# Row normalization: two 8 MB tiles with 64 KiB per partition in place of four 4 MB tiles with 32 KiB, and one of four squares on VectorE

## The chip, the cores and the metric

The kernel runs on one core of one Trainium2 chip. The metric is the device time of one execution in microseconds (us), as a median over several runs. The span of a profile, from its first to its last instruction, is shorter than the measured time by 1.7 to 1.8 us.

## The reference

```python
# x: 1024 x 4096 float32, eps = 1e-12
norm = np.sqrt(np.sum(x ** 2, axis=-1, keepdims=True) + eps)
return (x / norm).astype(np.float32)
```

16.78 MB come in from HBM, the chip's main memory, and 16.78 MB go out to it. A row can be scaled only when it has been squared and summed as a whole.

## The kernel before

Four tiles of 128 partitions with two whole rows each. All loads are issued first, on the SP queue. Then for each tile ACT squares and sums two rows, ACT takes the square root, VectorE (DVE) takes the reciprocal and scales both rows in place, and SP issues the store. Each tile has its own buffer in SBUF, the on-chip memory, so nothing ever waits for a free one: the four loads are issued one behind the other, from 0.73 to 2.1 us.

```python
R = 2
n_tiles = N // (P * R)                       # 4
x = x.rearrange("(t p r) d -> t p (r d)", p=P, r=R)
...
for i in range(n_tiles):                     # all loads
    xt = io.tile([P, R, D], mybir.dt.float32)
    nc.sync.dma_start(out=xt.rearrange("p r d -> p (r d)"), in_=x[i])
    xts.append(xt)
for i in range(n_tiles):
    ...
    for r in range(R):
        nc.scalar.activation(out=sq, in_=xt[:, r], func=Square,
                             accum_out=ssq[:, r : r + 1])
    nc.scalar.activation(out=rstd, in_=ssq, func=Sqrt, bias=eps_t)
    nc.vector.reciprocal(out=rstd, in_=rstd)
    for r in range(R):
        nc.vector.tensor_scalar_mul(out=xt[:, r], in0=xt[:, r],
                                    scalar1=rstd[:, r : r + 1])
    nc.sync.dma_start(out=out_t[i], in_=xt.rearrange("p r d -> p (r d)"))
```

Of the kernel before, what the change touches and what calls it, by code (L numbers as in the profile page):

```python
# [1 line left out]

# [4 lines left out]


@with_exitstack  # L10
def kernel(
    ctx: ExitStack,
    tc: tile.TileContext,
    x: bass.AP,
    axis: bass.AP,
    eps: bass.AP,
    out: bass.AP,
):
    nc = tc.nc
    P = nc.NUM_PARTITIONS  # L20

    assert isinstance(axis, int) and axis in (-1, len(x.shape) - 1)
    eps = float(eps)

    x = x.flatten_outer_dims()
    out_flat = out.flatten_outer_dims()
    N, D = x.shape
    assert N % P == 0

    R = 2  # L30
    n_tiles = N // (P * R)
    x = x.rearrange("(t p r) d -> t p (r d)", p=P, r=R)
    out_t = out_flat.rearrange("(t p r) d -> t p (r d)", p=P, r=R)

    io = ctx.enter_context(tc.tile_pool(name="io", bufs=n_tiles))
    scratch = ctx.enter_context(tc.tile_pool(name="scratch", bufs=1))
    stats = ctx.enter_context(tc.tile_pool(name="stats", bufs=4))

    sq = scratch.tile([P, D], mybir.dt.float32)
    eps_t = scratch.tile([P, 1], mybir.dt.float32)  # L40
    nc.vector.memset(eps_t, eps)  # L41

    xts = []
    for i in range(n_tiles):
        xt = io.tile([P, R, D], mybir.dt.float32)
        nc.sync.dma_start(out=xt.rearrange("p r d -> p (r d)"), in_=x[i])  # L46
        xts.append(xt)

    for i in range(n_tiles):
        xt = xts[i]  # L50
        ssq = stats.tile([P, R], mybir.dt.float32)
        for r in range(R):
            nc.scalar.activation(  # L53
                out=sq,
                in_=xt[:, r],
                func=mybir.ActivationFunctionType.Square,
                accum_out=ssq[:, r : r + 1],
            )

        rstd = stats.tile([P, R], mybir.dt.float32)  # L60
        nc.scalar.activation(  # L61
            out=rstd,
            in_=ssq,
            func=mybir.ActivationFunctionType.Sqrt,
            bias=eps_t,
        )
        nc.vector.reciprocal(out=rstd, in_=rstd)  # L67

        for r in range(R):
            nc.vector.tensor_scalar_mul(  # L70
                out=xt[:, r], in0=xt[:, r], scalar1=rstd[:, r : r + 1]
            )
        nc.sync.dma_start(out=out_t[i], in_=xt.rearrange("p r d -> p (r d)"))


# [1 line left out]
_INS = ['x', 'axis', 'eps']  # L77
_OUTS = [((1024, 4096), 'float32')]
#: Inputs that are plain numbers.
_NUMBERS = {'axis': -1, 'eps': 9.999999960041972e-13}  # L80


# [26 lines left out]
```

## Time and profile before

| | before |
|---|---|
| time, median of the first 3 runs | 84.22 us (84.21 to 84.26) |
| span of the profile | 82.5 us |
| DMA packets | 1152, of which 1024 of 32 KiB |
| DMA busy, mean of 16 engines | 96% |
| ACT busy, DVE busy | 41%, 23% |
| loads landed | 13.04, 22.76, 32.48, 42.97 us |
| stores issued, first and last | 27.0 and 55.6 us |

The DMA row counts. Its 96% say that hardly anything but the transfer itself can set the time. A packet is here one partition's share of a tile, 32 KiB in one piece (4 tiles x 128 partitions, in and out, make 1024); such a piece is called a descriptor below. The other 128 packets have 4 bytes and take 9 ns; each of the eight transfers has 16 of them, at its end. They are called semaphore packets below. What is left to argue about is in single microseconds: the start, the end, and the place where loads give way to stores. For these no summary view is fine enough, and the single packet records of the trace were read as well: start, length and size of each packet on each engine. The lines of the views are shown in the prediction. The packet records stand in no view and don't name their engine: packets were strung together to 16 engines by the end of one and the start of the next.

### The profile page before, as it was taken

The page shows a single profiled execution, that of the slowest core. Times are in us where ns is not written, and L with a number is a line of the kernel's source. Part 1 is how long each engine was busy: PE and PEld are TensorE (multiplying, and loading weights), DVE is VectorE, ACT ScalarE, POOL GpSimd, SP SyncE. Part 2 cuts the span into 40 slices and gives each one's busy share as a digit, 9 for nine tenths or more (in the row PEclk, how much of TensorE's full clock was granted, in tenths as well). Part 3 has the DMA queues.
Part 4 walks back from the last instruction along what each step waited for, and adds up shares of the span by engine and source line. Part 5 has one row for each costly group of instructions (what it writes and reads, how often), then busy time and mean ns, then how long its engine had stood idle before and what let it go on. Part 6 is the DMA issues. An engine that isn't in the chain of part 4 may idle for free.

```text
span 82.5 us, 98 instructions
## 1 busy us (share of the span) xinstructions
DVE 19.2 (23%) x13; ACT 33.4 (41%) x22; POOL 0.2 (0%) x4
## 2 busy tenths in 40 slices
DVE  0000000000299019910498003990000000000000
ACT  6000006999799982999519996000000000000000
POOL 0000000000000000000000000000000000000000
DMA  6689998996999899899979989998998998899890
GB/s 175 286 365 445 508 397 365 508 461 302 508 493 397 381 508 413 350 508 461 302 302 461 493 381 397 508 413 350 508 445 381 445 508 381 381 508 413 365 493 0
DMA packets 1152, 33.55 MB, mean 407 GB/s; under 512 B 128, under 2 KB 128, under 8 KB 128
## 3 DMA queue, kind: packets, MB, share of 16 engines
q1 hardware_dynamic: 1152, 33.55, 96.0%
HBM read 16.78 MB, written 16.78 MB: 407 GB/s over the span
## 4 chain that ended last, share of the span: by engine, by line
DMA 50%; ACT 9%; DVE 3%; DVEq 3%; SPq 1%; issue 0%
DMA xt<-in_x_dram 50%; ACT sq L53 9%; DVE xt L70 3%; DVEq L104 3%; SPq L46 1%; ACT rstd L61 0%; DVE rstd L67 0%
## 5 line engine op out<-in xcount | busy, mean ns | idle before, releaser
L53 ACT ACTIVATE sq<-xt 128x4096 f32<-128x4096 f32 x8 | 28.9, 3617 | 16.5 <-DMA xt<-in_x_dram 16.4
L70 DVE TENSOR_SCALAR xt<-xt,rstd 128x4096 f32<-128x4096 f32 x8 | 18.5, 2350 | 0.1
L67 DVE RECIPROCAL rstd<-rstd 128x2 f32<-128x2 f32 x4 | 0.7, 166 | 35.5 <-ACT rstd L61 35.5
L53 ACT ACT_TABLE_LOAD x1 | 1.3, 1283 | 0.7 <-PEq L90 0.7
L53 ACT ACTIVATION_READ_ACCUMULATOR sq<-xt 128x1 f32 x8 | 1.5, 186 | 0.0
L61 ACT ACT_TABLE_LOAD x1 | 1.3, 1283 | 0.0
L61 ACT ACTIVATE rstd<-ssq,eps_t 128x2 f32<-128x2 f32 x4 | 1.2, 296 | 0.1
L41 DVE MEMSET eps_t<- 128x1 f32 x1 | 0.1, 59 | 0.8 <-PEq L90 0.8
L90 POOL MEMSET const-bfloat16-1.0<- 128x1 bf16 x1 | 0.1, 102 | 0.0
L90 POOL MEMSET const-uint8-127<- 128x1 uint8 x1 | 0.1, 102 | 0.0
L90 POOL MEMSET const-float32-0.0<- 128x1 f32 x1 | 0.1, 99 | 0.2 <-issue 0.2
L90 POOL MEMSET const-float32-1.0<- 128x1 f32 x1 | 0.1, 99 | 0.0
## 6 DMA issues: line engine op xcount, KB each, us to landing
xt<-in_x_dram SPq DMA_DIRECT2D x4, 4096.0 KB, 26.2
out_dram<-xt SPq DMA_DIRECT2D x4, 4096.0 KB, 26.4
```

What stands on the lines that cost most here:

```text
L41: nc.vector.memset(eps_t, eps)
L46: nc.sync.dma_start(out=xt.rearrange("p r d -> p (r d)"), in_=x[i])
L53: nc.scalar.activation(out=sq, in_=xt[:, r], func=mybir.ActivationFunctionType.Square, accum_out=ssq[:, r : r + 1],)
L61: nc.scalar.activation(out=rstd, in_=ssq, func=mybir.ActivationFunctionType.Sqrt, bias=eps_t,)
L67: nc.vector.reciprocal(out=rstd, in_=rstd)
L70: nc.vector.tensor_scalar_mul(out=xt[:, r], in0=xt[:, r], scalar1=rstd[:, r : r + 1])
L90: nc = _bacc.Bacc("TRN2", target_bir_lowering=False, num_devices=1)
L104: with _tile.TileContext(nc) as tc:
```

## The change

Its intent: fewer, larger descriptors and transfers, and a shorter way from landing to store for the larger tile, by giving one square in four to VectorE, which has time. The core of the diff:

```diff
-    R = 2
+    R = 4
...
+    def square_dve(self, r):
+        self.nc.vector.scalar_tensor_tensor(
+            out=sq_v, in0=self.x[:, r], scalar=1.0, in1=self.x[:, r],
+            op0=ALU.mult, op1=ALU.mult,
+            accum_out=self.ssq[:, r : r + 1])
...
+    for i, g in enumerate(groups):          # two tiles
+        g.square_dve(R - 1)
+        g.square_act(0)
+        g.norm(0)                           # sqrt on ACT, reciprocal on DVE
+        g.scale(0)
+        g.square_act(1)
+        g.norm(1)
+        g.norm(R - 1)
+        g.scale(1)
+        g.scale(R - 1)
+        g.square_act(2)
+        g.norm(2)
+        g.scale(2)
+        nc.sync.dma_start(out=out_t[i], in_=g.flat())
```

More of the change, by code (lines that the diff above doesn't have):

```diff
@@ L7, with __init__, flat, square_act @@
 from concourse._compat import with_exitstack
+ACT_F = mybir.ActivationFunctionType
+ALU = mybir.AluOpType
+F32 = mybir.dt.float32
+class RowGroups:
+    def __init__(self, nc, io, stats, scratch, D, R, eps_t):
+        self.nc = nc
+        self.P = nc.NUM_PARTITIONS
+        self.R = R
+        self.D = D
+        self.eps_t = eps_t
+        self.scratch = scratch
+        self.x = io.tile([self.P, R, D], F32, name="xt")
+        self.ssq = stats.tile([self.P, R], F32, name="ssq")
+        self.rstd = stats.tile([self.P, R], F32, name="rstd")
+    def flat(self):
+        return self.x.rearrange("p r d -> p (r d)")
+    def square_act(self, r):
+        sq_a = self.scratch["act"]
+        self.nc.scalar.activation(
+            out=sq_a,
+            in_=self.x[:, r],
+            func=ACT_F.Square,
+            accum_out=self.ssq[:, r : r + 1],
+        )
+    def square_dve(self, r):
+        sq_v = self.scratch["dve"]
+        self.nc.vector.scalar_tensor_tensor(
+            out=sq_v,
+            in0=self.x[:, r],
+            scalar=1.0,
+            in1=self.x[:, r],
+            op0=ALU.mult,
+            op1=ALU.mult,
+            accum_out=self.ssq[:, r : r + 1],
+        )
+    def norm(self, r, n=1):
+        self.nc.scalar.activation(
+            out=self.rstd[:, r : r + n],
+            in_=self.ssq[:, r : r + n],
+            func=ACT_F.Sqrt,
+            bias=self.eps_t,
+        )
+        self.nc.vector.reciprocal(
+            out=self.rstd[:, r : r + n], in_=self.rstd[:, r : r + n]
+        )
+    def scale(self, r):
+        self.nc.vector.tensor_scalar_mul(
+            out=self.x[:, r], in0=self.x[:, r], scalar1=self.rstd[:, r : r + 1]
+        )
 @with_exitstack
@@ L27 @@
     N, D = x.shape
-    assert N % P == 0
-    R = 2
+    R = 4
+    assert N % (P * R) == 0
     n_tiles = N // (P * R)
-    x = x.rearrange("(t p r) d -> t p (r d)", p=P, r=R)
+    x_t = x.rearrange("(t p r) d -> t p (r d)", p=P, r=R)
     out_t = out_flat.rearrange("(t p r) d -> t p (r d)", p=P, r=R)
     io = ctx.enter_context(tc.tile_pool(name="io", bufs=n_tiles))
-    scratch = ctx.enter_context(tc.tile_pool(name="scratch", bufs=1))
-    stats = ctx.enter_context(tc.tile_pool(name="stats", bufs=4))
@@ L39 @@
-    sq = scratch.tile([P, D], mybir.dt.float32)
-    eps_t = scratch.tile([P, 1], mybir.dt.float32)
+    scratch_pool = ctx.enter_context(tc.tile_pool(name="scratch", bufs=1))
+    stats = ctx.enter_context(tc.tile_pool(name="stats", bufs=n_tiles))
+    eps_t = scratch_pool.tile([P, 1], F32)
     nc.vector.memset(eps_t, eps)
-    xts = []
+    sq_act = scratch_pool.tile([P, D], F32)
+    sq_dve = scratch_pool.tile([P, D], F32)
+    scratch = {"act": sq_act, "dve": sq_dve}
+    groups = []
     for i in range(n_tiles):
-        xt = io.tile([P, R, D], mybir.dt.float32)
-        nc.sync.dma_start(out=xt.rearrange("p r d -> p (r d)"), in_=x[i])
-        xts.append(xt)
@@ L49 @@
-    for i in range(n_tiles):
-        xt = xts[i]
-        ssq = stats.tile([P, R], mybir.dt.float32)
-        for r in range(R):
-            nc.scalar.activation(
-                out=sq,
-                in_=xt[:, r],
-                func=mybir.ActivationFunctionType.Square,
-                accum_out=ssq[:, r : r + 1],
-            )
-        rstd = stats.tile([P, R], mybir.dt.float32)
-        nc.scalar.activation(
-            out=rstd,
-            in_=ssq,
-            func=mybir.ActivationFunctionType.Sqrt,
-            bias=eps_t,
-        )
-        nc.vector.reciprocal(out=rstd, in_=rstd)
-        for r in range(R):
-            nc.vector.tensor_scalar_mul(
-                out=xt[:, r], in0=xt[:, r], scalar1=rstd[:, r : r + 1]
-            )
-        nc.sync.dma_start(out=out_t[i], in_=xt.rearrange("p r d -> p (r d)"))
+        g = RowGroups(nc, io, stats, scratch, D, R, eps_t)
@@ L77 @@
+        nc.sync.dma_start(out=g.flat(), in_=x_t[i])
+        groups.append(g)
+    for i, g in enumerate(groups):
[12 more added lines that the diff above has]
+        nc.sync.dma_start(out=out_t[i], in_=g.flat())
 _INS = ['x', 'axis', 'eps']
```

## The prediction

Passages that rested on rules or figures which no trace or run of this case shows are cut from it, and the cuts are marked. Terms of the sum went with them. The sum came to 84.22 - 0.3 = 83.9 us, and to 84.0 with 0.1 for the rivals. Of the 0.3, the cost of the 32 packets that each engine saves is cut, and the 4 x 9 ns of semaphore packets are left; if a data packet costs as much of its own as a semaphore packet takes in the trace, 9 ns, the cut term is 32 x 9 ns = 0.29 us. The 2418 ns forecast for a packet of 64 KiB came from the same cut figures; with the trace alone, 2 x 1213 - 9 = 2417 is near it. Rival B had a slower square, whose length is cut with the sum that led from it to a late store and to 84.9.

> **What bounds the kernel now.** I read the page first, for who is busy:
>
> ```profile
> span 82.5 us, 98 instructions
> DVE 19.2 (23%) x13; ACT 33.4 (41%) x22; POOL 0.2 (0%) x4
> DVE  0000000000299019910498003990000000000000
> ACT  6000006999799982999519996000000000000000
> DMA  6689998996999899899979989998998998899890
> q1 hardware_dynamic: 1152, 33.55, 96.0%
> ```
>
> ACT works 41% of the span, DVE 23%, and both are silent in the last third. The 16 DMA engines are busy in every slice but the last. So the kernel is one transfer of 33.55 MB (16.78 in, 16.78 out) with all arithmetic beside it.
>
> The chain of waits that ended last says "DMA 50%" and then ACT and DVE, which could mislead. In order of time it runs
>
> ```profile
> 2.11 40.86 DMA xt<-in_x_dram
> 42.99 3.72 ACT sq L53 x2
> 51.00 2.35 DVE xt L70
> 53.36 2.26 DVEq L104
> ```
>
> and stops at 55.6 us, where the last store is issued. The 26 us from there to the end are a store that waits in the queue behind other stores, and the chain does not show them. That the arithmetic between 43 and 55.6 us is not what the end waits for is seen in the stretches cut at the landings of the four loads (13.04, 22.75, 32.47, 42.96), at the issue of the last store (55.6) and at its landing (81.7). Columns: stretch, length, busy time of DVE, ACT, POOL, clock, DMA share, GB/s:
>
> ```profile
> 0.00:1.73 1.73, 0.06 (x1) 1.00 (x1) 0.20 (x4) 1.00 0.00 0
> 1.73:13.04 11.31, 0.00 (x0) 0.28 (x1) 0.00 (x0) 1.00 1.02 417
> 13.04:22.75 9.71, 0.56 (x2) 9.00 (x6) 0.00 (x0) 1.00 1.00 432
> 22.75:32.47 9.72, 6.07 (x4) 7.71 (x5) 0.00 (x0) 1.00 1.00 432
> 32.47:42.96 10.49, 5.55 (x5) 7.71 (x5) 0.00 (x0) 1.00 1.01 400
> 42.96:55.60 12.64, 6.94 (x4) 7.71 (x5) 0.00 (x0) 1.00 1.01 436
> 81.70:82.50 0.80, 0.00 (x0) 0.00 (x0) 0.00 (x0) 1.00 0.00 0
> ```
>
> While the fourth tile is computed, the DMA moves 436 GB/s: stores of earlier tiles fill the time. The packet records of the trace (start and length of each DMA packet) say how fast: a 32 KiB packet takes 1213 ns on its engine, with a few exceptions, back to back. Each engine moves 64 of them: 64 x 1.213 = 77.6 us. The rest of the 82.5 us: 1.73 before the first packet; about 0.8 because an engine's first packet takes about 2.0; about 0.8 because its last load packet, at 40.1 to 42.6 where loads give way to stores, also takes about 2.0; 0.1 of semaphore packets (9 ns each); 0.3 to 0.4 from the last packet to landing; and 0.8 of closing waits. The measured time, 84.22, is 1.7 more than the span; I carry that as a constant.
>
> [...] The trace: 32768 bytes in 1213 ns is 27.0 GB/s, 432 over 16 engines[...]
>
> **The change part by part.** Bytes, queue and order stay: all loads, then all stores, on one queue.
>
> *Descriptors.* 32 packets of 64 KiB per engine in place of 64 of 32 KiB. [...] 4 x 9 ns of semaphore packets. Call it **-0.3 us**, if 64 KiB is really one packet.
>
> *Fewer, later stores.* The first store now needs all of an 8 MB tile. Its load lands when the second 4 MB load did, and ACT began on that at 22.78. I carry durations over: square 3.62, with accumulator read 3.71 (3.74 from start to start); sqrt 0.30; table load 1.28, once, after the first square as before; reciprocal 0.17; scale 2.35 (2.27 start to start); handovers about 0.03. The VectorE square has no row; [...] estimate 4.5.
>
> Tile 0, ACT: square 0 22.78 to 26.49, table to 27.80, sqrt to 28.12; square 1 to 31.85, sqrt 1 and 3 to 32.49; square 2 to 36.22, sqrt to 36.54. DVE: its square to 27.3; reciprocal and scale 0, 28.15 to 30.7; reciprocals 1 and 3 until 32.7; scales 1 and 3 to 37.35; reciprocal and scale 2 to 39.9. Store issued at **39.95**. From issue to first packet a load took 1.0 us (0.73 to 1.73), so data is available from 40.95. The engines finish their loads at about 42.1 to 42.6. Margin 1.1 us or more: no gap.
>
> Tile 1 lands about 42.9. ACT: sqrt 0 at 47.0, sqrts 1 and 3 at 51.4, sqrt 2 at 55.4. DVE: square to 47.5, scale 0 to 50.05, reciprocals to 51.6, scales 1 and 3 to 56.2, reciprocal and scale 2 to 58.8. Store issued **58.85**, able to start about 59.85. The first store holds the engines from about 42.3 for 16 x 1.213 = 19.4 us, until 61.7. Margin about 1.8 us: no gap.
>
> So the chain from landing to store grows from about 12.6 to 16 us, the margin before the last store shrinks from some 16 us (55.6 against about 72) to about 2, and neither moves the end. *One square on VectorE* takes 2 x 3.7 us off ACT and adds 2 x 4.5 to DVE, and is what keeps the margins positive: with a fourth square on ACT each store would come nearly 4 us later. Its worth in time, alone, is zero while DMA is the bound.
>
> Sum: 84.22 - 0.3 = 83.9. I add 0.1 for the rivals below, which mostly point upward: **84.0 us**.
>
> **The rivals.**
> *A: descriptors don't matter.* If [...] the hardware cuts 64 KiB in two again, nothing is saved: 84.2. For it: [...] I have one packet size only. Against it: the same 9 ns on semaphore packets.
> *B: a gap before a store (DVE becomes the bound at the seam).* [...] That makes about 84.9. Even this stays within 2%.
> *C: the seam between loads and stores.* The 0.8 us that an engine loses there now occur with the store queued 15 us ahead; then, only about 1 us ahead. If what is queued is fetched later, the loss may grow to some 1.5 us (84.7) or go. The start of the run, with nothing queued before, cost the same 0.8, so I expect no growth.
> *D: 64 KiB packets move slower*, from HBM or by coarser balance between the engines. Nothing in the trace supports it: the engines ended within 0.6 us of each other and all packets in steady state are alike. A fall of 2% in rate would be 1.6 us, 85.8.
> *E: a real gain.* To be 2% faster, 1.7 us must go. [...] it would have to come from the start, the seam or the end, none of which the change touches.
>
> **Range and chances.** Centre 84.0. The low end, 83.6, is the packet saving with half of the seam's 0.8 us gone as well; the high end, 84.9, is rival B. Outside 2% (below 82.5 or above 85.9) needs E, or D or a coincidence of B and C: 2% and 4%. Within 2%: 94%.
>
> **What would show it.** Right: a queue row of about 576 packets (4 x 128 data and 64 semaphore), 33.55 MB, DMA busy in all slices but the last; 64 KiB packets near 2418 ns; stores issued near 40 and 59 us; the last issue to landing some 22 us instead of 26; ACT busy near 27 us (33.4 less two squares, plus four sqrts), DVE near 29 (19.2 plus two squares and four reciprocals). Wrong: a slice with lower DMA share at 41 to 43 or 60 to 62 us (B or C), a VectorE square well above 5 us (B), 1152 packets still (A), or packets over 2426 ns (D).

## The result, and the profile after

83.87 us median (83.78 to 84.03, 5 runs), against 84.25 us (84.21 to 84.36) for the kernel before. The ratio is 0.9954, with a 95% interval of 0.9942 to 0.9965. A ratio here is the mean time of one kernel's fast runs over that of the other's of the same rounds, so it is not quite the ratio of the medians. It is 0.4% faster: clear of noise, and "the same" at 2%.

The page after, for who is busy. The rows of digits are the busy share in tenths over 40 slices of the span:

```profile
span 82.2 us, 93 instructions
DVE 28.6 (35%) x21; ACT 26.4 (32%) x22; POOL 0.2 (0%) x4
DVE  0000000000099599977029995999200000000000
ACT  6000000000099999940029999950000000000000
DMA  9299974999995699999199997599999669999920
q1 hardware_dynamic: 576, 33.55, 95.6%
L42 DVE SCALAR_TENSOR_TENSOR sq_dve<-xt 128x4096 f32<-128x4096 f32 x2 | 8.8, 4424 | 25.9 <-DMA xt<-in_x_dram 25.9
```

The packets are halved, the bytes are the same, and ACT and DVE have about changed places. The dips in the DMA row are no idle engines, for the packet records follow each other without a gap. The packets now last 2.4 us, longer than a slice of 2.05; the engines start theirs nearly together (the last load packets at 38.53 to 39.12), and a packet is evidently counted where it starts, for the stretches from the first packet on show DMA shares up to 1.08. With such long packets the row can't be read for small gaps.

The timeline after, at the places that matter (start, length, engine, line, operation; in brackets the idle time before it and who ended it):

```profile
22.58 3.62 ACT L33 ACTIVATE sq_act<-xt 128x4096 f32<-128x4096 f32 x1 [20.56 <-DMA xt<-in_x_dram]
...
27.60 0.48 ACT L53 ACTIVATE rstd<-ssq,eps_t 128x1 f32<-128x1 f32 x2
...
27.99 3.60 ACT L33 ACTIVATE sq_act<-xt 128x4096 f32<-128x4096 f32 x1
28.12 2.35 DVE L64 TENSOR_SCALAR xt<-xt,rstd 128x4096 f32<-128x4096 f32 x1
...
30.58 2.35 DVE L64 TENSOR_SCALAR xt<-xt,rstd 128x4096 f32<-128x4096 f32 x1
...
38.55 19.88 SPq L122 DMA_DIRECT2D out_dram<-xt  x2
42.73 3.62 ACT L33 ACTIVATE sq_act<-xt 128x4096 f32<-128x4096 f32 x1 [6.80 <-DMA xt<-in_x_dram]
```

Before, the stores' row was

```profile
27.00 28.97 SPq L73 DMA_DIRECT2D out_dram<-xt  x4
```

The first store is issued at 38.55 us in place of 27.0, and the second at 58.1. The scale at 30.58 is that of the VectorE row: it runs while ACT still squares, earlier than the source has it, because the emitted order differs from the source's: two square roots stand at 27.60, ahead of the square at 27.99. The stretches between landings (stretch, length, busy time of DVE, ACT, POOL, clock, DMA share, GB/s):

```profile
22.55:42.71 20.16, 14.32 (x10) 13.26 (x11) 0.00 (x0) 1.00 0.98 416
42.71:62.09 19.38, 14.23 (x10) 11.87 (x10) 0.00 (x0) 1.00 1.00 433
```

The second load of 8 MB takes 20.16 us and the first store of 8 MB 19.38. Before, the last 4 MB load took 10.49 where the one ahead of it took 9.72. In both kernels the load ahead of the first store is too slow. The packet records show it on the last packets of each engine: before they have 0.87 us too much per engine (mean of 16), after 0.46. I call this the **loss at the seam**: the time by which load packets exceed the usual 1213 or 2418 ns just ahead of the first store.

Where the time came from, from the packet records of the two profiled runs, as means over the 16 engines:

| | before | after | difference |
|---|---|---|---|
| first packet starts | 2.05 | 1.93 | -0.12 |
| excess of the first packets | 0.64 | 0.69 | +0.05 |
| data packets | 64 x 1.213 = 77.63 | 32 x 2.418 = 77.38 | -0.26 |
| loss at the seam | 0.87 | 0.46 | -0.41 |
| semaphore packets, overlap of records | -0.16 | -0.10 | +0.06 |
| last data packet ends, mean engine | 81.03 | 80.35 | -0.68 |
| last data packet ends, last engine | 81.33 | 81.05 | -0.28 |

The mean engine gains 0.68 us. The end of the last one, for which the core waits, moves by only 0.28: in the run after it still had a loss at the seam of 0.90, about twice the mean. The packet lengths are as forecast. Neighbouring records overlap by 4 ns, though, and with fewer packets there is less overlap, so packets, semaphores and overlap together save 0.20 (-0.26 and +0.06). The seam, which the forecast held constant, moved by more than that. Each column is one profile; a second one of the changed kernel has a loss of 0.24 (below). The experiments ask what the seam depends on.

### The profile page after: what moved, and what is told of

The parts are those of the page before. It is cut to its first block, busy times and chain, and to the rows that moved or that the text cites. A ratio compares the mean times of both kernels' runs of the same rounds, so it can differ in the third digit from the quotient of the medians.

```text
span 82.2 us, 93 instructions
## 1 busy us (share of the span) xinstructions
DVE 28.6 (35%) x21; ACT 26.4 (32%) x22; POOL 0.2 (0%) x4
## 4 chain that ended last, share of the span: by engine, by line
DMA 51%; ACT 9%; DVE 9%; SPq 0%; issue 0%
DMA xt<-in_x_dram 51%; ACT sq_act L33 9%; DVE xt L64 9%; ACT rstd L53 1%; SPq L106 0%; DVE rstd L59 0%
## 5 line engine op out<-in xcount | busy, mean ns | idle before, releaser
L33 ACT ACTIVATE sq_act<-xt 128x4096 f32<-128x4096 f32 x6 | 21.6, 3608 | 27.4 <-DMA xt<-in_x_dram 27.4
L42 DVE SCALAR_TENSOR_TENSOR sq_dve<-xt 128x4096 f32<-128x4096 f32 x2 | 8.8, 4424 | 25.9 <-DMA xt<-in_x_dram 25.9
L53 ACT ACTIVATE rstd<-ssq,eps_t 128x1 f32<-128x1 f32 x8 | 2.1, 288 | 0.1
L59 DVE RECIPROCAL rstd<-rstd 128x1 f32<-128x1 f32 x8 | 1.3, 159 | 2.4 <-ACT rstd L53 2.4
L33 ACT ACTIVATION_READ_ACCUMULATOR sq_act<-xt 128x1 f32 x6 | 1.1, 185 | 0.0
```

The lines of the kernel that those rows point to most:

```text
L33: self.nc.scalar.activation(out=sq_a, in_=self.x[:, r], func=ACT_F.Square, accum_out=self.ssq[:, r : r + 1],)
L42: self.nc.vector.scalar_tensor_tensor(out=sq_v, in0=self.x[:, r], scalar=1.0, in1=self.x[:, r], op0=ALU.mult, op1=ALU.mult, accum_out=self ...
L53: self.nc.scalar.activation(out=self.rstd[:, r : r + n], in_=self.ssq[:, r : r + n], func=ACT_F.Sqrt, bias=self.eps_t,)
L59: self.nc.vector.reciprocal(out=self.rstd[:, r : r + n], in_=self.rstd[:, r : r + n])
```

## The experiments

Twelve runs in three sittings (ten kernels, the changed kernel once more, and one repeat), each timed beside the kernel before (its medians were 84.25, 84.31 and 84.29 us). All give correct results except one.

### Descriptor size alone

*The changed kernel with 32 KiB descriptors*, label d32_in_8mb. A gap of 64 unused elements in SBUF after two rows ends the descriptor, and its packets had 32 KiB; HBM order, tiles and arithmetic stay.

```diff
-        self.x = io.tile([self.P, R, D], F32, name="xt")
+        self.x = io.tile([self.P, 2, 2 * D + 64], F32, name="xt")
...
-    x_t = x.rearrange("(t p r) d -> t p (r d)", p=P, r=R)
+    x_t = x.rearrange("(t p h q) d -> t p h (q d)", p=P, h=2, q=R // 2)
```

> The changed kernel with its 8 MB tiles, stores and issue times as they are, but 32 KiB per descriptor (64 unused elements after two rows in SBUF end the descriptor). Theory, a fixed cost of some 8 ns per packet: 64 data packets per engine of 1213 ns again in place of 32 of 2418, so 32 x 8 ns = 0.26 us are given back: about 84.1 to 84.2 us. Rival, the gain came from fewer and larger transfers or from a cheaper seam between loads and stores: stays at 83.9. The seam should show in the packet records whether it goes with packet size or with the time at which the first store is queued.

Measured: 84.03 us, ratio 0.9965 (0.9949 to 0.9982).

*The kernel before with 16 KiB descriptors*, label d16_in_4mb, by the same means.

```diff
-        xt = io.tile([P, R, D], mybir.dt.float32)
+        xt = io.tile([P, R, D + 64], mybir.dt.float32)
...
-    x = x.rearrange("(t p r) d -> t p (r d)", p=P, r=R)
+    x = x.rearrange("(t p r) d -> t p r d", p=P, r=R)
```

> The kernel before with 16 KiB per descriptor in place of 32. Theory of a fixed cost per packet: [...] about 84.75 us. Rival, the rate is what it is and packets cost nothing of their own: 606.5 ns and 84.25 us.

The sum for the packets is cut, for it used a rate that no trace shows. From the lengths in the two profiles, 8 ns of its own per packet (2 x 1213 - 2418) would be 64 x 8 ns = 0.51 us more.

Measured: 84.71 us, ratio 1.0054 (1.0039 to 1.007). The page's queue row shows the packets doubled:

```profile
q1 hardware_dynamic: 2176, 33.55, 95.8%
```

The packet lengths decide. A packet of 16, 32 and 64 KiB takes 611, 1213 and 2418 ns (medians). From 32 to 64 KiB it is 1205 ns more, which is 27.2 GB/s per engine; a packet then has 1213 - 1205 = 8 ns of its own, and from 16 to 32 KiB the same sum gives 9. These are lengths, and each record overlaps the next by 4 ns. From start to start, which is what counts for the end, packets of the three sizes follow each other after 607, 1209 and 2414 ns, and the same sums leave 4 to 5 ns per packet. So a fixed cost per packet is **shown**, of 4 to 5 ns from start to start. The 8 ns of the lengths would be worth 32 x 8 = 0.26 us between the two kernels; from start to start it is 64 x 1.209 - 32 x 2.414 = 0.13.

The two times, though they came out near what was expected, don't show it by themselves. In these kernels the first packet started at 2.18 and 2.19 us in place of 1.74 (the issue of a load with two runs per partition took 0.59 to 0.70 us in place of 0.38 to 0.53), and the loss at the seam fell to 0.16 (32 KiB) and 0.38 (16 KiB, summed over the last load tile). In d16_in_4mb the later start (+0.41 in the mean engine), the first packets (+0.07), the packets (128 x 0.611 - 64 x 1.213 = +0.58), their overlap (-0.27) and the seam (0.38 - 0.87 = -0.49) add up to 0.3 to 0.4, and the last engine ends 0.44 later: near the 0.5 that was expected from the packets alone, but by chance. In d32_in_8mb the start and the seam (+0.55 and -0.30) cancel in part as well, so its 84.03 decides nothing between 84.1 and its rival's 83.9.

### The square on VectorE, in both kernels

*The changed kernel with all squares on ACT*, label act_only_8mb.

```diff
-        g.square_dve(R - 1)
+        g.square_act(R - 1)
```

> The changed kernel with its fourth square back on ACT. Theory, margins of 1 to 2 us before each store: the first store is issued near 42.2 us in place of 38.55 and its data could start near 43.2, 1.2 to 1.8 us after the engines have finished their loads (41.4 to 42.0): a gap in the DMA row at that place, and about 85.3 us (84.9 to 85.6). The second store, issued near 61.4, should then just come in time. Rival, what the chain of waits suggests, that the last tile's whole arithmetic is on the path: 3.7 us more, 87.5. Second rival, the queue hides all of it: 83.9.

Measured: 85.06 us, ratio 1.0102 (1.0084 to 1.0119), 1.2 us slower than the changed kernel by the medians. The timeline's row of the stores, with the start of the first:

```profile
42.30 18.23 SPq L122 DMA_DIRECT2D out_dram<-xt  x2
```

The stretch from the end of the last load packet to the start of the first store packet:

```profile
41.52:43.14 1.62, 0.75 (x1) 1.25 (x1) 0.00 (x0) 1.00 0.00 0
```

All 16 engines stand still for 1.62 us, with a DMA share of 0.00, until a store issued at 42.30 reaches them 0.84 us later. This is the gap that the margin keeps away. Per engine it is 1.90 us on average, and against it the loss at the seam is gone: none of the last load packets is longer than 2420 ns. In the last engine, which sets the end, the records give 82.07 against 81.05 us, 1.0 later; the times say 1.2. The rival that the chain of waits suggests, 87.5, falls.

*The kernel before with one square of four on VectorE*, label dve_sq_4mb.

```diff
         for r in range(R):
+            if r == 1 and i % 2 == 1:
+                nc.vector.scalar_tensor_tensor(out=sq_v, in0=xt[:, r], scalar=1.0,
+                    in1=xt[:, r], op0=mult, op1=mult, accum_out=ssq[:, r : r + 1])
+                continue
             nc.scalar.activation(
```

> The kernel before with one of four squares on VectorE (row 1 of tiles 1 and 3) and nothing else changed. Theory, arithmetic is far inside the DMA's shadow there: 84.2 us, with the last store issued some 3 us earlier and waiting longer. Rival, the VectorE square shortens the path after the last load: up to 3 us less.

Measured: 84.32 us, ratio 1.0003 (0.9988 to 1.0017). Alone the square is worth nothing; it matters in the changed kernel, where without it a gap opens. Its last store was issued at 54.5 in place of 55.6 us, about 1 us earlier and not 3 as expected, and that earned nothing.

### The seam: when the first store is queued

The runs so far suggested that the loss goes with how early the store is in the queue, or else with the size of packets or tiles. Early and late stores were tried with both sizes.

*The changed kernel, first tile stored as it came*, label early_store_8mb (result wrong).

```diff
+    nc.sync.dma_start(out=out_t[0], in_=groups[0].flat())
     for i, g in enumerate(groups):
+        if i == 0:
+            continue
```

> The changed kernel with the first tile stored as it came, right after landing (wrong result on purpose), so that a 64 KiB store is queued 18 us ahead of the seam. Theory, the loss goes with the packet size when the store is queued long ahead (0.33 us with 16 KiB, 0.87 to 1.1 with 32): 1.7 to 2.2 us in place of 0.45, and about 85.3 us. Rival, the loss is about 0.9 whatever the packet: 84.3. Second rival, the early store changes nothing: 83.9.

Measured: 84.46 us, ratio 1.0015 (1.0 to 1.003). The store:

```profile
22.80 0.35 SPq L110 DMA_DIRECT2D out_dram<-xt  x1
```

The stretch from the first landing to the second:

```profile
22.78:43.08 20.30, 0.00 (x0) 0.00 (x0) 0.00 (x0) 1.00 1.01 413
```

The second load takes 20.30 us with no arithmetic running at all. The loss is 1.18 us: more than the changed kernel's 0.46, so the early store costs, but not the 1.7 to 2.2 of a loss in proportion to the packet, so that expectation missed; its first rival, 0.9 whatever the packet, is nearer. And since ACT and DVE are idle here, the loss doesn't need any contention with them.

*The changed kernel, first store later by one needless VectorE instruction*: labels later_c_8mb (352 elements), later_a_8mb (1024), later_a_again (the same kernel once more), later_b_8mb (2480).

```diff
         g.norm(2)
+        if i == 0:      # only to delay the first store
+            nc.vector.tensor_scalar_mul(out=sq_dve[:, :1024],
+                in0=g.x[:, 2, :1024], scalar1=g.rstd[:, 2:3])
         g.scale(2)
```

> The changed kernel with one needless scale of 1024 elements on VectorE ahead of the last scale of tile 0: first store issued 0.75 us later, near 39.3, its data able to start near 40.3, still before the loads end (41.4 to 41.6 when nothing disturbs them). Theory of the queued time: the loss at the seam shrinks from 0.45 to 0.2 or less and the time to about 83.6. Rival, the loss is the same or any delay of the store is a loss: 83.9 to 84.6.

> As later_a_8mb with 2480 elements: first store issued 1.5 us later, near 40.05, data able to start near 41.05, just before the loads end. Theory: no loss at the seam and hardly a gap: about 83.5 us, the best of all. Rival, a gap of 0.3 to 0.7 us opens on some engines and eats it: 84.0.

> The changed kernel with a needless scale of 352 elements: first store issued 0.4 us later, near 38.95, between the changed kernel (38.55, loss 0.46) and later_a_8mb (39.29, loss 0.00). Theory, the loss grows with the time for which the ready store overlaps the last load packet: 0.1 to 0.3 us and 83.4 to 83.7 us. Rival, a threshold: either as later_a (83.25) or as the changed kernel (83.87).

> later_a_8mb once more: 0.987 of the kernel before, 83.2 us, if it was not chance, and no loss at the seam.

Measured: later_a_8mb 83.24 us, ratio 0.9869 (0.9851 to 0.9887), and again 83.15 us, 0.9864 (0.9845 to 0.9882); later_c_8mb 83.35 us, 0.9886 (0.9867 to 0.9905); later_b_8mb 83.53 us, 0.9903 (0.9884 to 0.9921). The needless work makes the kernel faster. later_a_8mb did better than expected (83.6), and later_b_8mb came at the expected time but is not the best of all, for a gap of 0.21 us opened. later_c_8mb was to tell a gradual loss from a threshold: at 0.05 us, where 0.1 to 0.3 was expected, it is nearly as later_a_8mb, so this is not settled. The timeline of later_a_8mb around the first store:

```profile
36.12 0.75 DVE L123 TENSOR_SCALAR sq_dve<-xt,rstd 128x1024 f32<-128x1024 f32 x1
36.91 2.35 DVE L64 TENSOR_SCALAR xt<-xt,rstd 128x4096 f32<-128x4096 f32 x1
39.29 0.35 SPq L127 DMA_DIRECT2D out_dram<-xt  x1
```

Its stretches between landings, for the second load and the first store:

```profile
22.50:41.83 19.33, 15.07 (x11) 13.26 (x11) 0.00 (x0) 1.00 1.00 434
41.83:61.19 19.36, 14.22 (x10) 11.87 (x10) 0.00 (x0) 1.00 1.00 433
```

0.75 us more on VectorE, a store at 39.29 in place of 38.55, and the second load takes 19.33 us, as long as the store after it. The loss is 0.01 us, and there is no gap: the first store packets start at 41.03 to 41.49, where the last load packets end. By the medians the time fell by 0.63 us, and by 0.76 in the repeat; the last engine of the changed kernel lost 0.90 and 0.64 us at the seam in its two profiles, which is of that order.

*The changed kernel once more*, label after_again, as the control.

> The changed kernel once more, as a control for the runs beside it: 0.995 to 0.996 of the kernel before, 83.9 us, and a loss at the seam of 0.3 to 0.6 us in the packet records.

Measured: 83.91 us (83.52 to 84.16), ratio 0.9949 (0.9923 to 0.9974). The profiled run was its fastest, 83.52, and its loss at the seam was 0.24, somewhat below what was expected.

### The same in the kernel before: two aims missed

*Needless scales on VectorE in the kernel before*, label late_store_4mb; then, with the amount mended, label jit_store_4mb.

```diff
+        if i == 0:      # late_store_4mb: ahead of the reciprocal, five times
+            nc.vector.tensor_scalar_mul(out=pad, in0=xt[:, 0], scalar1=ssq[:, 0:1])
+        if i == 0:      # jit_store_4mb: behind it, one of D // 4 and five of D elements
+            nc.vector.tensor_scalar_mul(out=pad[:, :n], in0=xt[:, 0, :n],
+                                        scalar1=rstd[:, 0:1])
```

> The kernel before, 32 KiB packets, with five needless scales on VectorE so that the first store is issued near 38.4 us in place of 27.0, about 2 us before the engines finish their loads; the later stores still come before the queue needs them. In the runs so far the last load packet of each engine was too long by 0.87 us (before) and 1.10 (the square moved, both with the store queued 15 us ahead), but by 0.16 with 32 KiB packets in 8 MB tiles and a store issued 2 us ahead. Theory, the loss at the seam depends on how long the store has been queued: it falls below 0.4 us here and the time to about 83.7. Rival, it depends on the size of the transfers: it stays near 0.9 and the time at 84.25.

> late_store_4mb with the needless scales where they hold: the kernel before, 32 KiB packets and four tiles, with its first store issued near 39.5 us, ready near 40.4, one microsecond before the loads end. The run before it missed its aim (issued at 34.0, loss at the seam 0.92), so packet size and queued time were not told apart. Theory, the loss at the seam comes from a store that is ready before the last load packet is nearly done, whatever the size: it falls below 0.2 us and the time to 83.4 to 83.6 us, with no change of descriptors or tiles. Rival, 32 KiB packets or four tiles lose 0.9 at the seam in any case: 84.25.

Measured: late_store_4mb 84.34 us, ratio 1.0007 (0.9985 to 1.0029); jit_store_4mb 84.56 us, 1.0029 (1.001 to 1.0048). Neither store came when it was meant to. In late_store_4mb two of the needless scales ran while VectorE waited anyway, and the store was issued at 34.02:

```profile
34.02 22.22 SPq L80 DMA_DIRECT2D out_dram<-xt  x4
```

The loss stayed at 0.92, though this store was queued 7 us later than that of the kernel before. In jit_store_4mb the timeline has it at 41.53, after two scales in a row (from 36.89 on) where the forecast, 39.5, had counted on one:

```profile
41.53 13.45 SPq L80 DMA_DIRECT2D out_dram<-xt  x4
```

The stretch between the last load packet and the first store packet there:

```profile
41.52:42.38 0.86, 0.86 (x1) 0.39 (x1) 0.00 (x0) 1.00 0.09 38
```

The loss is gone here too, all last load packets taking 1213 ns, but a gap of 1.15 us per engine stands in its place. So with 32 KiB packets in four tiles the loss also vanishes when no store is ready, which rules out that it belongs to that size. That the kernel before would gain its 0.87 us with a store at the right moment was not shown: it was never hit.

### All runs in the order of the first store

From the timelines and the packet records. Loss and gap are means per engine in the profiled run.

| kernel | packet | first store issued | loss at the seam | gap | time, median |
|---|---|---|---|---|---|
| dve_sq_4mb | 32 KiB | 26.77 | 1.10 | 0 | 84.32 |
| before | 32 KiB | 27.00 | 0.87 | 0 | 84.25 |
| d16_in_4mb | 16 KiB | 27.59 | 0.38 | 0 | 84.71 |
| late_store_4mb | 32 KiB | 34.02 | 0.92 | 0 | 84.34 |
| d32_in_8mb | 32 KiB | 39.09 | 0.16 | 0 | 84.03 |
| jit_store_4mb | 32 KiB | 41.53 | 0.00 | 1.15 | 84.56 |
| early_store_8mb | 64 KiB | 22.80 | 1.18 | 0 | 84.46 |
| after | 64 KiB | 38.55 | 0.46 | 0 | 83.87 |
| after_again | 64 KiB | 38.67 | 0.24 | 0 | 83.91 |
| later_c_8mb | 64 KiB | 39.14 | 0.05 | 0 | 83.35 |
| later_a_8mb | 64 KiB | 39.29 | 0.01 | 0 | 83.24 |
| later_a_again | 64 KiB | 39.44 | 0.01 | 0 | 83.15 |
| later_b_8mb | 64 KiB | 40.18 | 0.00 | 0.21 | 83.53 |
| act_only_8mb | 64 KiB | 42.30 | 0.00 | 1.90 | 85.06 |

In the 64 KiB rows the loss falls as the store comes later, and is gone from 39.3 us on, when a store becomes ready (0.84 to 1.0 us after its issue, by the three runs with a gap) about a microsecond before the last load packets end at 41.0 to 41.6. Later than that, the gap grows. That the moment of the store sets the loss is **shown** by these runs, whose transfers differ in nothing else. It is not how long the store has been queued: with 32 KiB packets in four tiles the loss is 1.10, 0.87 and 0.92 for stores at 26.77, 27.00 and 34.02, without a fall. Among such early stores the loss also differs with the packet, 0.38 at 16 KiB against 1.18 at 64, by one profile each. Why an engine's last load packets take longer when a store is ready behind them is **not shown**: the store packets that follow have their usual length (1213 ns before, 2418 to 2432 after), so the lost time is not repaid. That the profiled run of the changed kernel with the smaller loss was the faster one (0.24 and 83.52 us against 0.46 and 83.96) fits the loss making the spread of its times; two runs don't prove it.

## Why the prediction was right

The time was forecast at 84.0 us, 83.6 to 84.9, with 94% for "the same"; it came out at 83.87 and again at 83.91. The verdict rests on the bound, which held; that the total came so near rests in part on luck, as the seam shows. Step by step:

- **DMA is the bound, arithmetic is in its shadow.** Right. Moving a square in the kernel before changed nothing (1.0003), and the changed kernel's last tile has a chain of 15.4 us behind its landing (42.71 to 58.1) that costs nothing: the store ahead of it moves at 433 GB/s until 62.09. The forecast's account of the 82.5 us adds up to only 82.2; for one thing, it took the first engine's start, 1.73, where the mean is 2.05.
- **The packet cost.** Right in kind, too large in size. 2418 ns was forecast and measured, so rivals A (descriptors don't matter) and D (64 KiB packets move slower) fall. But the cost of a packet, 8 ns by the measured lengths, is 4 to 5 ns from start to start, and the saving is 0.20 us with semaphores and overlap, where 0.3 was forecast.
- **The VectorE square.** Right, but it rested on the estimate of 4.5 us, which no trace had shown: 4.42 was measured, and 0.08 for the accumulator. Rival B, which needs a square well above 5 us, falls.
- **The margins.** Right in kind: no gap before either store. The stores came at 38.55 and 58.1 where 39.95 and 58.85 were forecast. The first came early mainly because the scale of the VectorE row ran while ACT was still squaring. In the second tile the order is the forecast one; about 0.2 of its 0.75 is the earlier landing, the rest small differences along the chain. That the square on VectorE keeps the first margin positive was shown by taking it away: 1.62 us of standstill.
- **The seam.** This is the step that failed. Rival C said of it that "the start of the run, with nothing queued before, cost the same 0.8, so I expect no growth", the sum held it constant, and rival E said that the start, the seam and the end were places "none of which the change touches". The change moved the first store by 11.5 us, and the loss at the seam fell from 0.87 to 0.46 (0.24 in the second profile). In the mean engine this was the larger part of the gain: 0.41 of 0.68 us. Nor was the start of the run a measure for it: in act_only_8mb the first store packets after the standstill took 2449 to 2465 ns, hardly more than usual. The forecast of the total held because the end is that of the last engine, which moved by only 0.28 us. Nothing in the prediction said so: that is luck. The 0.1 added for rivals was not needed, for 83.9 without it is what came.
- **What would show it wrong** named a low DMA share near 41 to 43 us. With packets longer than a slice the row dips without any gap, so this sign was badly chosen; the packet records and the stretches between landings were needed.

The experiments also led past both kernels: with its first store 0.75 us later, the changed kernel took 83.24 and 83.15 us, 1.3% to 1.4% under the kernel before.

## What to carry to other kernels

When a transfer bounds a kernel, count its packets and look for the microseconds that are not packets: the start, the end, and the change from loads to stores on one queue. A store wants to be ready neither long before the loads end, where it slowed the last load packets by up to 1.2 us here, nor after, where the engines stand still (0.21 to 1.90 us per engine in the three runs with a gap); about a microsecond ahead was best here, with 64 KiB packets, the only ones with which that moment was hit. Work moved between engines was worth nothing by itself here (ratio 1.0003), but it was what kept a store in time (issued at 38.55 us, and without it at 42.30), so compute the margin of each store, not the busy shares.
